# Splitting the modulated tokens where they are produced, and loading them in ten split slots

## The chip, the core and the metric

The kernel runs on one NeuronCore of a Trainium2 chip. The metric is the time of one execution in microseconds on the device. A core has five engines that run their own instruction lists in order and wait for each other by semaphores: TensorE (PE, matrix products), VectorE (DVE), ScalarE (ACT), GpSimd (POOL) and SyncE (SP). In this kernel SP issues every DMA, and it too works through one list in order: an issue that waits holds back all issues behind it.

## The reference

Two layers over 2048 latent tokens and 256 context tokens of 1024 features, in float32:

```python
for i in range(DEPTH):
    ml = layer_norm(xl) * (1.0 + sc_l) + sh_l          # the same for the context tokens
    parts = split(ml @ w_in[i])                        # one wide projection
    oa = gdn_branch(...)   # gated DeltaNet: short convolution, gates, chunked scan in both directions
    ob = na_branch(...)    # neighbourhood attention on a 64 wide grid
    oc = gla_branch(...)   # gated linear attention in both directions
    y = concat(norm(oa) * silu(z_a), ob * silu(z_b), norm(oc) * silu(z_c)) @ w_out[i]
    xl = layer_norm(alpha * xl + gate * y) * ln_g[i] + ln_b[i]
```

## The kernel before

The 2304 tokens (context first) are 18 tiles of 128 tokens, or 6 blocks of 384 (BLK). M, the normalised and modulated tokens, transposed to features by tokens, is the input of the projection. It lies in DRAM, one tensor M0 to M5 for each block, float32, 128 partitions by 8 feature slices (KD) by 384 tokens. `modulate` makes a tile of it: PE transposes the normalised tile (L165), ACT scales and shifts it into `m` (L168), and a DMA stores `m` (L170). In layer 0 that is a stage of its own ahead of the projection (`stage_p1`); for layer 1 the output stage of layer 0 (`Out.run`) calls it after each of its tiles.

The projection needs more precision than one pass of TensorE in float32r gives, so each operand is split in a leading part with float32r's significand and the rest, and three products are summed (`dense_mm`, L202). The class `Dense` streams M five times for each layer: pass 1 with the columns of GLA (while GLA's blocks run), pass 2 with those of the neighbourhood attention, passes 3 and 4 with keys, queries and values of two heads of DeltaNet each (the conv passes: a convolution of five taps on DVE, L654, then SiLU and layouts), pass 5 with DeltaNet's z columns (while the scan is being set up). In each pass `Dense.block` loads a block in four raw tiles of two feature slices and splits each of them: ACT makes the leading part `mh` (L191), POOL or DVE in turn the rest `ml` (L194). There are two slots for raw tiles and four for each of the parts, so that one block fills all of the split slots:

```python
raw = pool.tile([128, 2, BLK], F32, tag="mraw", name="mraw")        # two slots
nc.sync.dma_start(raw, self.M[b][:, 2 * h:2 * h + 2])
for lst, tag in ((mh, "mh"), (ml, "ml")):
    lst.append(pool.tile([128, 2, BLK], F32R, tag=tag, name=tag, bufs=4))
split_(e, mh[h], ml[h], raw, nc.scalar, nc.vector if h % 2 else nc.gpsimd)
```

The order of the instructions of every engine is set when the kernel is built, by a scheduler that works with estimated times and priorities; the splits have a high priority. Memory is handed out by pools; a pool that is opened where another one lay waits for that one's last work. The weights' raw tiles (`raw`, L229) are split likewise (`wh`, `wl`).

## Time and profile before

| what | value |
|---|---|
| median of 3 runs | 4035.41 us |
| the 3 runs | 4031.47, 4035.41, 4062.93 us |
| span of the profiled execution | 4030.6 us |
| busy: PE, PEld, DVE, ACT, POOL | 90%, 78%, 69%, 46%, 28% of the span |
| mean granted TensorE clock | 0.905 of full speed |
| DMA moved | 674.38 MB, 167 GB/s on average |
| layer 0: pass 1, pass 2 | 73 to 326 us, 326 to 668 us |
| layer 0: conv passes | 668 to 903 us, 903 to 1122 us |
| layer 0: pass 5, scan and attention, output stage | 1122 to 1290, 1290 to 1810, 1810 to 2140 us |
| layer 1: pass 1, pass 2 | 2140 to 2342 us, 2342 to 2681 us |
| layer 1: conv passes, pass 5 | 2681 to 2906, 2906 to 3088, 3088 to 3250 us |

The profiled execution's span, first to last instruction, is 4030.6 us; the time of an execution has a little more around it: the fastest of the three runs is 0.9 us longer than this span, and the median 4.8 us longer. The stages are cut where the loads of a pass's blocks begin; stages overlap at the cuts. Busy shares are means over stages with different limits, so what counts is which wait ends last within a stage.

### The profile page before, as it was taken

What the parts mean: (1) busy time and instruction counts of PE and PEld (TensorE: products, weight loads), DVE (VectorE), ACT (ScalarE), POOL (GpSimd) and SP (SyncE); (2) the same over time, 40 slices, a digit from 0 to 9 for tenths busy, and PEclk for the clock granted to TensorE, in tenths of its full rate; (3) what the DMA queues carried; (4) which work ended last, traced back from release to release, by engine and by line L of the source; (5) the groups of instructions that cost most, each with busy time, mean ns of one, the idle gap of its engine ahead of it and who ended that gap; (6) DMA issues with size and microseconds to landing.
All of it is one profiled execution on the core that took longest, in us unless ns stands there. A gap on an engine that the chain in (4) does not pass through costs nothing.

```text
span 4030.6 us, 77205 instructions
## 1 busy us (share of the span) xinstructions
PE 3609.5 (90%) x27270; PEld 3133.3 (78%) x27270; DVE 2765.4 (69%) x7584; ACT 1847.2 (46%) x4628; POOL 1142.5 (28%) x1334
## 2 busy tenths in 40 slices
PE   5999999888998999997898989998899989889788
PEld 2777778877887888996676768887898778879676
DVE  7455653899987667447776466438999865754587
ACT  6534322456543544546555342324565434445442
POOL 2121212554223322321332121125324231232133
PEclk6979879899999978998899887999999987989899
DMA  8523226654566868666545232266554776785743
GB/s 285 163 75 118 82 70 186 171 170 145 167 202 193 243 193 224 213 188 210 176 140 167 88 98 70 91 194 170 161 159 146 247 218 178 212 229 164 230 146 110
DMA packets 646265, 674.38 MB, mean 167 GB/s; under 512 B 184830, under 2 KB 524662, under 8 KB 645878
## 3 DMA queue, kind: packets, MB, share of 16 engines
q1 hardware_dynamic: 645878, 669.44, 55.2%
q8 instruction: 216, 3.54, 0.4%
q14 instruction: 171, 1.40, 0.1%
HBM read 472.98 MB, written 196.28 MB: 166 GB/s over the span
## 4 chain that ended last, share of the span: by engine, by line
PE 42%; DVE 26%; DMA 16%; ACT 6%; issue 5%; POOL 2%; SPq 2%; DVEq 0%; ACTq 0%; POOLq 0%
PE p L202 18%; DVE acc L654 5%; PE p L1250 3%; DMA gb<-GR 2%; PE py L202 2%; DMA raw<-in_w_in 2%; DMA mraw<-M 2%; PE pv L1015 1%; PE pd L1022 1%; PE po L1035 1%; DVE mix L1356 1%; DMA OA<-o 1%; PE pk L1004 1%; PE pA L491 1%; DVE gb L858 1%
## 5 line engine op out<-in xcount | busy, mean ns | idle before, releaser
L202 PE MATMUL p<-ml,wh 128*128 128x384 f32 (+1 forms) x1824 | 648.9, 356 | 49.7 <-POOL ml L194 35.2
L202 PE MATMUL p<-mh,wh 128*128 128x384 f32 (+1 forms) x1824 | 644.3, 357 | 33.6 <-ACT mh L191 9.9
L202 PE MATMUL p<-mh,wl 128*128 128x384 f32 (+1 forms) x1824 | 639.9, 351 | 0.6 <-DVE wl L194 0.6
L194 POOL TENSOR_TENSOR ml<-mraw,mh 128x768 fp32r<-128x768 f32 x120 | 248.7, 2072 | 632.6 <-ACT mh L191 602.1
L202 PEld LDWEIGHTS p<-ml,wh 128*128 128x128 f32 (+1 forms) x1824 | 354.8, 195 | 80.5 <-POOL ml L194 45.4
L654 DVE SCALAR_TENSOR_TENSOR acc<-pre,cw,acc 128x384 f32<-128x384 f32 (+1 forms) x576 | 400.4, 712 | 15.1 <-ACT acc L652 12.2
L202 PEld LDWEIGHTS p<-mh,wh 128*128 128x128 f32 (+1 forms) x1824 | 353.4, 195 | 64.1 <-ACT mh L191 15.8
L202 PEld LDWEIGHTS p<-mh,wl 128*128 128x128 f32 (+1 forms) x1824 | 354.9, 195 | 12.3 <-issue 1.6
L202 PE MATMUL p<-wh,mh 128*128 128x512 f32 (+1 forms) x848 | 343.9, 406 | 14.2 <-DVE zt L1266 9.3
L202 PE MATMUL p<-wl,mh 128*128 128x512 f32 (+1 forms) x848 | 340.0, 401 | 5.5 <-DVE wl L194 5.5
L202 PE MATMUL p<-wh,ml 128*128 128x512 f32 (+1 forms) x848 | 341.8, 405 | 1.8 <-POOL ml L194 1.6
L191 ACT CAST mh<-mraw 128x768 fp32r<-128x768 f32 x240 | 197.9, 833 | 140.0 <-DMA mraw<-M 109.1
L202 PE MATMUL py<-wh,mh 128*128 128x512 f32 x544 | 222.4, 410 | 17.6 <-ACT mh L1365 14.4
L202 PE MATMUL py<-wl,mh 128*128 128x512 f32 x544 | 218.3, 402 | 0.3 <-DVE wl L1303 0.3
L202 PE MATMUL py<-wh,ml 128*128 128x512 f32 x544 | 213.4, 404 | 4.3 <-DVE ml L1366 4.3
L997 POOL TENSOR_TENSOR kd<-kk,eD 128x256 f32<-128x256 f32 x144 | 90.1, 627 | 437.0 <-DMA kk<-KK 147.3
L202 PEld LDWEIGHTS p<-wh,mh 128*128 128x128 f32 x848 | 164.9, 195 | 53.0 <-DVE zt L1266 12.1
L202 PEld LDWEIGHTS p<-wh,ml 128*128 128x128 f32 x848 | 165.0, 195 | 40.0 <-POOL ml L194 3.1
L202 PEld LDWEIGHTS p<-wl,mh 128*128 128x128 f32 x848 | 165.5, 195 | 38.8 <-DVE wl L194 6.0
L1388 POOL TENSOR_TENSOR y<-y,g 128x1024 f32<-128x1024 f32 x32 | 77.0, 2408 | 412.5 <-ACT y L1387 412.5
L194 DVE TENSOR_TENSOR ml<-mraw,mh 128x768 fp32r<-128x768 f32 x120 | 134.8, 1123 | 71.8 <-ACT mh L191 71.7
L1229 ACT ACTIVATE w<-w,mn 128x696 f32<-128x696 f32 (+2 forms) x136 | 112.9, 831 | 135.6 <-DVE mn L1226 135.0
(323 smaller groups left out, 8947.5 us busy)
## 6 DMA issues: line engine op xcount, KB each, us to landing
mraw<-M SPq DMA_DIRECT2D x240, 384.0 KB
kk<-KK SPq DMA_DIRECT2D x144, 512.0 KB
raw<-in_w_in SPq DMA_DIRECT2D x104, 256.0 KB
w<-in_w_mod SPq DMA_DIRECT2D x96, 256.0 KB
M<-m SPq DMA_DIRECT2D x36, 512.0 KB
KK<-kq SPq DMA_DIRECT2D x96, 192.0 KB
KK<-kvt SPq DMA_DIRECT2D x48, 384.0 KB
kq<-KK SPq DMA_DIRECT2D x72, 256.0 KB
```

The source lines that it names most:

```text
L191: eng_hi.copy(hi, src)
L194: eng_lo.tensor_tensor(lo, src, hi.bitcast(F32), op=ALU.subtract)
L202: e.nc.tensor.matmul(p, x(k), y(k), start=n == 0, stop=n == 3 * KD - 1)
L491: nc.tensor.matmul(pA[jb * s:jb * s + s, i, ib * s:ib * s + s], KQ[s][hs, 0, t0 + jb * s:t0 + jb * s + s], KQ[s][hs, 1, t0 + ib * s:t0 + i ...
L654: nc.vector.scalar_tensor_tensor(acc[:, :n], pre[:, k:k + n], w(kind, k), acc[:, :n], op0=ALU.mult, op1=ALU.add)
L858: nc.vector.scalar_tensor_tensor(E[:, d, h], gb[:, d, h], self.G[:, d, c, h0 + h:h0 + h + 1], e.mats[:, 1 + d], op0=ALU.subtract, op1=ALU.min)
L997: nc.gpsimd.tensor_tensor(kd, kv[:, :, 0], self.eD[:, d, c, h0:h0 + 2].unsqueeze(2).to_broadcast([128, 2, 128]), op=ALU.mult)
L1004: nc.tensor.matmul(pk[:, h], kq[:, h, 0], S[:, h], start=True, stop=True)
L1015: nc.tensor.matmul(pv[:, h], X[:, h], R[:, h], start=True, stop=True)
L1229: nc.scalar.activation(w[:, a, 0:256 + nk], w[:, a, 0:256 + nk], AF.Exp, bias=m[:, a:a + 1], scale=-1.0, accum_out=sm[:, a:a + 1])
L1250: nc.tensor.matmul(p[:, a], l, r, start=j == 0, stop=j == len(parts) - 1)
L1388: eng.tensor_tensor(y[:, s], y[:, s], self.g[:, 0, s], op=ALU.mult)
```

## The change

`modulate` now splits its tile: ACT copies each half of `m` to a float32r tile `mhi`, POOL subtracts that from `m` in place, and two DMAs store the two parts. M has a second axis for the parts. `Dense.block` loads the finished parts slice by slice, both parts of a feature slice in one load, into ten slots; nothing is split in the passes. The other lines of the diff only drop comments.

```diff
@@ modulate
-    nc.sync.dma_start(M[b][:, :, o:o + 128], m)
+    h = P.tile([128, KD, 128], F32R, tag="mhi", name="mhi")
+    l = m.bitcast(F32R)
+    for q in range(2):
+        s = slice(4 * q, 4 * q + 4)
+        nc.scalar.copy(h[:, s], m[:, s])
+        nc.gpsimd.tensor_tensor(l[:, s], m[:, s], h[:, s].bitcast(F32), op=ALU.subtract)
+    nc.sync.dma_start(M[b][:, 0, :, o:o + 128], h.bitcast(F32))
+    nc.sync.dma_start(M[b][:, 1, :, o:o + 128], m)
@@ Dense.block
-        mh, ml = [], []
-        for h in range(4):
-            raw = pool.tile([128, 2, BLK], F32, tag="mraw", name="mraw")
-            nc.sync.dma_start(raw, self.M[b][:, 2 * h:2 * h + 2])
-            for lst, tag in ((mh, "mh"), (ml, "ml")):
-                lst.append(pool.tile([128, 2, BLK], F32R, tag=tag, name=tag, bufs=4))
-            with e.tc.high_priority(PRI):
-                split_(e, mh[h], ml[h], raw, nc.scalar, nc.vector if h % 2 else nc.gpsimd)
-        return mh, ml
+        m = []
+        for k in range(KD):
+            m.append(self.mp.tile([128, 2, BLK], F32R, tag="mm", name="mm", bufs=MBUF))
+            self.e.nc.sync.dma_start(m[k].bitcast(F32), self.M[b][:, :, k])
+        return m
@@ Dense.run
-                dense_mm(e, p, lambda k: wh[:, k], lambda k: wl[:, k], lambda k: mh[k // 2][:, k % 2], lambda k: ml[k // 2][:, k % 2])
+                dense_mm(e, p, lambda k: wh[:, k], lambda k: wl[:, k], lambda k: m[k][:, 0], lambda k: m[k][:, 1])
@@ Layer.__init__
-        self.M = [d.tile([128, KD, BLK], F32, name=f"M{b}") for b in range(NB)]
+        self.M = [d.tile([128, 2, KD, BLK], F32, name=f"M{b}") for b in range(NB)]
```

The slots take as much memory as before (two raw and eight split tiles of 3 KB for each partition, now ten of 3 KB); the pools of `stage_p1` and of the output stage grow by the two buffers of `mhi`, 8 KB for each partition. The scheduler makes a new order of the whole program from this. Three places of it follow.

First place: SP's list at the start of layer 0, after the first stores of M. M_70 to M_75 are the six blocks of M; `raw` are raw weights; x is the input. Before:

```order
L170 DMA M_70<-m 1024x1x128
L179 DMA x<-in_x 128x1024
L229 DMA raw<-in_w_in 128x4x128 x2
L170 DMA M_71<-m 1024x1x128
L229 DMA raw<-in_w_in 128x4x128
L240 DMA mraw<-M_70 128x768 x2
L229 DMA raw<-in_w_in 128x4x128
L170 DMA M_71<-m 1024x1x128
```

SP's list of the changed kernel, where these weights (128x4x128: columns of k and q; 128x256: of v and z) now stand:

```order
L176 DMA M_75<-mhi 128x8x128
L177 DMA M_75<-m 128x8x128
L393 DMA b2c<-in_gla_b 128x2x1
L391 DMA w2p<-in_gla_w 16x128 x2
L237 DMA raw<-in_w_in 128x4x128 x4
L406 DMA rp<-in_rope 128x768
L410 DMA rc<-RC 32x384
L237 DMA raw<-in_w_in 128x256 x16
```

The loads of the weights of k, q, v and z have moved from between the first tiles' stores to behind the stores of the last tile of the last block.

Second place: PE's list at the start of layer 0. L165 are the transposes of `stage_p1`, eight for each tile; 48x384 is the first column group of pass 1, 128x384 those of k and q. Before:

```order
L165 MATMUL p<-ident,xn 128x128 x56
L202 MATMUL p<-mh,wh 48x384
L202 MATMUL p<-mh,wh 128x384
L202 MATMUL p<-ml,wh 48x384
L202 MATMUL p<-mh,wl 48x384
L202 MATMUL p<-mh,wh 48x384
```

PE's list of the changed kernel, from the end of the first column group of block 0 (the first group stands behind 44 transposes and between 12 more):

```order
L209 MATMUL p<-mm,wh 48x384 x2
L209 MATMUL p<-mm,wl 48x384
L372 MATMUL pt<-ident,r_1336 128x48 x3
L165 MATMUL p<-ident,xn 128x128 x88
L209 MATMUL p<-mm,wh 128x384 x2
L209 MATMUL p<-mm,wl 128x384
```

Before, products of k stood behind the transposes of seven tiles, and those of the other eleven tiles among the products; now all 144 transposes stand ahead of the first product of k.

Third place: DVE's list in the second conv pass of layer 0 (acc: convolution taps; ml: the split; X, A, xd: set-up of the scan). Before:

```order
L879 STREAM_TRANSPOSE xd<-X 32x192 x4
L654 SCALAR_TENSOR_TENSOR acc<-pre,cw,acc 128x384
L659 SCALAR_TENSOR_TENSOR vb<-th,acc 128x2
L659 SCALAR_TENSOR_TENSOR vb<-th,acc 128x382
L682 COPY kvt<-p 128x3x128
L654 SCALAR_TENSOR_TENSOR acc<-pre,cw,acc 128x384 x3
L659 SCALAR_TENSOR_TENSOR kq<-th,acc 128x2
L659 SCALAR_TENSOR_TENSOR kq<-th,acc 128x382
L687 TENSOR_SCALAR nv<-ss 128x6
L654 SCALAR_TENSOR_TENSOR acc<-pre,cw,acc 128x384
L194 TENSOR_TENSOR ml<-mraw,mh 128x768
```

DVE's list of the changed kernel in the same pass:

```order
L883 STREAM_TRANSPOSE xd<-X 32x192 x4
L867 SCALAR_TENSOR_TENSOR X<-pk,nW,gb 128x128
L658 SCALAR_TENSOR_TENSOR acc<-pre,cw,acc 128x384
L867 SCALAR_TENSOR_TENSOR X<-pk,nW,gb 128x128
L658 SCALAR_TENSOR_TENSOR acc<-pre,cw,acc 128x384
L869 TENSOR_TENSOR A<-pk,gb 128x256
L867 SCALAR_TENSOR_TENSOR X<-pk,nW,gb 128x128 x2
L663 SCALAR_TENSOR_TENSOR vb<-th,acc 128x2
L663 SCALAR_TENSOR_TENSOR vb<-th,acc 128x382
L658 SCALAR_TENSOR_TENSOR acc<-pre,cw,acc 128x384
```

The split is gone from between the taps. On SP's list the loads of a block in the passes now stand as two slices early and six in a row, each of which waits for PE to have read its slot for the last time.

## Rows read from the trace of the kernel before

**Rows 1.** Windows by stage: engines' busy us (instructions), granted clock, DMA share, GB/s.

```profile
668.00:903.00 235.00, 206.06 (x1056) 185.13 (x1055) 193.78 (x376) 110.68 (x256) 108.44 (x112) 0.92 0.65 179
903.00:1122.00 219.00, 195.67 (x1082) 177.73 (x1082) 203.85 (x530) 123.99 (x304) 79.10 (x83) 0.97 0.51 152
1810.00:2140.00 330.00, 275.48 (x1302) 225.14 (x1300) 251.92 (x785) 186.85 (x593) 85.21 (x36) 0.92 0.55 177
2681.00:2906.00 225.00, 199.00 (x1046) 181.13 (x1046) 182.38 (x368) 103.72 (x244) 94.93 (x101) 0.95 0.60 168
2906.00:3088.00 182.00, 175.10 (x1014) 168.48 (x1013) 174.99 (x517) 109.50 (x269) 54.89 (x58) 0.99 0.49 144
```

**Rows 2.** Chain of waits by line, conv passes: 668:903, 903:1122, 2681:2906, 2906:3088.

```profile
by line: DVE acc L654 26.8%; DMA raw<-in_w_in 11.7%; issue 8.1%; PE p L202 7.9%; DVE kq L659 5.5%; DVE nry L60 4.0%; DVE wl L194 3.6%; ACT acc L652 2.7%; DVE vb L659 2.6%; ACT wh L191 2.1%; DVE ml L194 2.1%; DVE nk L689 1.8%; DVE nra L58 1.
by line: DVE acc L654 21.6%; PE p L202 14.1%; issue 11.0%; DMA gb<-GR 5.7%; DVE ml L194 3.8%; DVE nry L60 3.7%; DVE vb L659 3.4%; POOL ml L194 2.9%; DVE nra L59 2.5%; ACT jk L685 2.5%; DVE kq L659 2.4%; DVE wl L194 2.2%; ACT kvt L697 2.1%; 
by line: PE p L202 23.4%; DVE acc L654 18.5%; issue 8.0%; DMA raw<-in_w_in 6.7%; DVE kq L659 4.6%; DMA tr<-RZ 3.7%; DVE wl L194 2.9%; DVE ml L194 2.4%; SPq L1123 2.3%; DVE vb L659 2.2%; POOL tb L1126 1.9%; ACT acc L652 1.8%; DMA w<-in_w_mod
by line: DVE acc L654 26.1%; issue 12.4%; PE p L202 12.3%; DMA mraw<-M 3.9%; DVE kq L659 3.8%; DVE ml L194 3.0%; DVE X L863 2.7%; DVE M L919 2.5%; DVE vb L659 2.4%; DVE gb L858 2.2%; DVE nry L60 1.9%; DMA gb<-GR 1.8%; ACT jk L685 1.8%; DVE 
```

**Rows 3.** Chain of waits by line: 73:326, 326:668, 1122:1290, 2140:2342, 2342:2681.

```profile
by line: PE p L202 52.1%; PE pA L491 4.7%; DMA mraw<-M 4.5%; PE p L165 2.6%; POOL ml L194 2.6%; PE pO L525 2.5%; POOL qkp L469 2.3%; ACT m L168 2.3%; DMA M<-m 2.2%; DVE a L446 2.1%; issue 2.0%; PE pD L473 1.8%; PE pB L498 1.8%; DVE a L441 1
by line: PE p L202 37.8%; issue 4.9%; PE pD L473 3.7%; PE pA L491 3.6%; PE pO L525 3.1%; DVE a L446 3.1%; POOL qkp L469 2.8%; DMA mraw<-M 2.8%; POOL ml L194 2.5%; DVE a L442 2.2%; PE pO L523 2.0%; PE pB L498 1.9%; DVE a L441 1.6%; DMA OC<-o
by line: PE p L202 45.0%; DMA gb<-GR 7.7%; DMA mraw<-M 7.4%; issue 3.8%; DVE gb L858 3.6%; DVE X L863 3.1%; DVE acc L654 2.7%; DVE xd L879 2.3%; PE pz L935 2.3%; DVE A L865 2.0%; PE px L941 1.5%; DVE tmp L918 1.4%; PE pq L675 1.4%; DVE M L9
by line: PE p L202 37.5%; DMA mraw<-M 5.3%; POOL ml L194 4.7%; issue 4.4%; PE pA L491 2.7%; ACT mh L191 2.6%; DVE a L446 2.6%; DMA raw<-in_w_in 2.4%; PE pD L473 2.3%; DVE a L441 2.3%; DVE A L511 2.2%; POOL qkp L469 2.1%; PE pO L525 1.7%; DV
by line: PE p L202 35.1%; DMA o<-OC 4.2%; PE pD L473 3.9%; DMA OC<-o 3.9%; DMA mraw<-M 3.6%; issue 3.6%; PE pA L491 3.5%; PE pO L525 2.9%; DVE a L446 2.7%; DVE G L508 2.5%; DVE A L511 2.5%; DVE a L442 2.0%; DVE a L441 1.8%; DVE a L443 1.7%;
```

**Rows 4.** Tile mraw: the splits, ns min/median/max, first and last start us.

```profile
L191 ACT CAST mh<-mraw x240: 814/834/879, 79.9 to 3236.8; 128x768 fp32r<-128x768 f32 x120
L194 POOL TENSOR_TENSOR ml<-mraw,mh x120: 1799/1846/6107, 80.9 to 3235.2; 128x768 fp32r<-128x768 f32 x120
L194 DVE TENSOR_TENSOR ml<-mraw,mh x120: 935/948/2595, 81.6 to 3238.5; 128x768 fp32r<-128x768 f32 x120
```

**Rows 5.** Timeline of POOL, then DVE, in layer 1's second conv pass: start us, us.

```profile
2933.34 2.30 POOL L194 TENSOR_TENSOR ml<-mraw,mh 128x768 fp32r<-128x768 f32 x1 [1.40 <-ACT mh L191]
...
2933.86 2.19 DVE L654 SCALAR_TENSOR_TENSOR acc<-pre,cw,acc 128x386 f32<-128x386 f32 x1
...
2936.59 0.61 DVE L654 SCALAR_TENSOR_TENSOR acc<-pre,cw,acc 128x386 f32<-128x386 f32 x1
```

**Rows 6.** Chain of waits in order of time, 0 to 135 us: start us, us.

```profile
58.03 4.56 DMA M<-m
...
70.94 5.64 DMA M<-m
...
76.69 2.90 ACT m L168 x8
...
83.33 5.16 PE p L202 x21
...
126.87 3.19 DMA mraw<-M
```

**Rows 7.** Groups kept apart by shape: count, busy us, mean ns.

```profile
L194 POOL TENSOR_TENSOR wml<-w,wmh 128x512 fp32r<-128x512 f32 x80 | 120.7, 1511 | 61.5 <-ACT wmh L191 41.4 <-ACT pre L645 11.0 <-ACT mh L191 3.2
L191 ACT CAST wmh<-w 128x512 fp32r<-128x512 f32 x96 | 59.0, 616 | 28.8 <-DMA w<-in_w_mod 11.1 <-POOL wml L194 8.8 <-DVE wml L194 5.4
```

**Rows 8.** DMA: GB/s in 40 slices of the span; an issue's size.

```profile
GB/s 285 163 75 118 82 70 186 171 170 145 167 202 193 243 193 224 213 188 210 176 140 167 88 98 70 91 194 170 161 159 146 247 218 178 212 229 164 230 146 110
...
M<-m SPq DMA_DIRECT2D x36, 512.0 KB
```

**Rows 9.** Longest pieces of the chain, whole span: a run of dense products.

```profile
3033.64 12.41 PE p L202 x70
```

More of the change, by code (lines that the diff above doesn't have):

```diff
@@ L206 @@
 PRI = 100000
+MBUF = 10
 class Dense:
@@ L235, in block @@
     def block(self, b):
-        e, nc, pool = self.e, self.e.nc, self.mp
-        mh, ml = [], []
-        for h in range(4):
-            raw = pool.tile([128, 2, BLK], F32, tag="mraw", name="mraw")
-            nc.sync.dma_start(raw, self.M[b][:, 2 * h:2 * h + 2])
-            for lst, tag in ((mh, "mh"), (ml, "ml")):
-                lst.append(pool.tile([128, 2, BLK], F32R, tag=tag, name=tag, bufs=4))
-            with e.tc.high_priority(PRI):
-                split_(e, mh[h], ml[h], raw, nc.scalar, nc.vector if h % 2 else nc.gpsimd)
-        return mh, ml
+        m = []
[3 more added lines that the diff above has]
+        return m
     def run(self, wp, chan, tok, bufs=1, after=None, width=None, raws=4, tw=None, w0=None):
@@ L262, in run @@
         for b in range(NB):
-            mh, ml = nxt if b == 0 else self.block(b)
+            m = nxt if b == 0 else self.block(b)
             for (wh, wl, wd), cb in cw:
                 p = ps.tile([wd, BLK], F32, tag="dn", name="p")
-                dense_mm(e, p, lambda k: wh[:, k], lambda k: wl[:, k], lambda k: mh[k // 2][:, k % 2], lambda k: ml[k // 2][:, k % 2])
+                dense_mm(e, p, lambda k: wh[:, k], lambda k: wl[:, k], lambda k: m[k][:, 0], lambda k: m[k][:, 1])
                 with e.tc.high_priority(PRI):
@@ L274, in run @@
                     s = slice(t * 128, (t + 1) * 128)
-                    dense_mm(e, p, lambda k: mh[k // 2][:, k % 2, s], lambda k: ml[k // 2][:, k % 2, s], lambda k: wh[:, k, :wd], lambda k: wl[:, k, :wd])
+                    dense_mm(e, p, lambda k: m[k][:, 0, s], lambda k: m[k][:, 1, s], lambda k: wh[:, k, :wd], lambda k: wl[:, k, :wd])
                     with e.tc.high_priority(PRI):
```

## Prediction

> **What bounds the kernel now.** I read the windows by stage first, to see in each which engine is full; then the chain of waits for the same windows, to see which waits end last; then the rows of the splits themselves and what they disturb; and last the start, in order of time. The windows show the conv passes to be DVE's: it is busy for 194 of 235, 204 of 219, 182 of 225 and 175 of 182 us [rows 1], and the convolution's taps alone hold 27, 22, 19 and 26% of their chains [rows 2]. Passes 1, 2 and 5 are PE's: dense products hold 35 to 52% of the chain [rows 3]. The splits stand on these chains, but in small pieces, and the start of layer 0, where M is made, is on PE's way as a whole: the first run of dense products begins at 83.3 us, behind the first stores of M [rows 6].
>
> **The change part by part.**
>
> *A. The splits in the passes go.* 240 casts, 120 POOL and 120 DVE subtractions leave [rows 4]. What counts is their share of the chain. Conv passes: DVE's ml has 2.1% of 235, 3.8% of 219, 2.4% of 225 and 3.0% of 182 us, that is 4.9 + 8.3 + 5.4 + 5.5 = 24.1 us, and POOL's ml 2.9% of 219 = 6.4 us [rows 2]; together 30.5 us. Passes 1 and 2: POOL's ml has 2.6% of 253, 2.5% of 342 and 4.7% of 202 us, 6.6 + 8.6 + 9.5 = 24.7 us, and ACT's mh 2.6% of 202 = 5.3 us [rows 3]; together 30.0 us. Names below the cut of these rows are not counted. In sum 60.5 us. In the conv passes PE is next: 36 groups of 24 products are 864, at 12.41 us for 70 [rows 9] 153 us, against windows of 182 to 235 us, so each pass could give 29 us or more before PE binds.
>
> *B. POOL no longer holds DVE up.* A POOL split ran from 2933.34 for 2.30 us; the tap that began at 2933.86 took 2.19 us where the one at 2936.59 took 0.61 [rows 5]. It lost 1.58 us. The four conv passes have 48 such POOL splits, so DVE may get back anything from 0 to 48 x 1.58 = 76 us. Of DVE's 755 us there [rows 1] the named DVE pieces of the chain hold 46.4% of 235, 39.6% of 219, 30.6% of 225 and 44.6% of 182 us, 346 us [rows 2], or 46%. I take that share, 35 us; it is nearer to the row than either end.
>
> The rule behind this is in the Trainium skill, page "SBUF — State Buffer", section "Who interferes with whom": a VectorE instruction with two SBUF inputs and a GpSimd instruction that reads SBUF exclude each other, and the later one waits for the whole of the other. This trace agrees: POOL's split ended at 2935.64 and the tap at 2936.05 [rows 5]. The rule speaks against the change too, since the new subtractions run on POOL; that is a rival below.
>
> *C. The loads double.* 240 loads of 384 KB become 480. No load has a split behind it, but two slices of a block are loaded ahead and six wait for PE to have read their slots; before, two raw tiles, half a block, were ahead. SP waits with them, and the stores of keys and values, the raw weights and the scan's rows queue behind. Loads have 4.5% of 253, 2.8% of 342, 7.4% of 168, 5.3% of 202, 3.6% of 339 and 3.9% of 182 us of the chain, 11.4 + 9.6 + 12.4 + 10.7 + 12.2 + 7.1 = 63.4 us [rows 2, 3]. Between the last read of a slot and the first use of its new content stand some 30 products on PE's list, 5.3 us at the rate above [rows 9], and a load took 3.19 us when it was alone [rows 6]. So most are covered. From below, the 63 us could vanish; from above, double. I take no change: the cover is longer than the load, but six in a row share the queues.
>
> *D. The output stage of layer 0.* Each of 18 tiles gets two casts of 0.62 us and two POOL subtractions of 1.51 us [rows 7], and a second store of 512 KB [rows 8]. ACT is busy for 187 of 330 us there, DVE for 252 [rows 1]. Casts cost between 0 and 18 x 1.23 = 22 us; the subtractions, by holding DVE, between 0 and 36 x 1.51 = 54 us. ACT idles for 43% of the time and POOL's ends are off the way, so I take 15 us, near the lower end.
>
> *E. The start of layer 0.* This is where order counts. Before, the weights of k, q, v and z were loaded between the first tiles' stores, and PE took up dense products after seven tiles. Now SP issues these weights behind the store of the last tile, and PE's list has all 144 transposes ahead of k's first product. The cover that is lost: eleven tiles of `stage_p1` ran beside dense products. The first store was issued at 58.03 us [rows 6]; the first low part now comes a cast pair and a subtraction later, at 58.0 + 1.2 + 1.5 = 60.8 us. A tile's pace: `m` has two buffers, each held for 2.90 us of writing, 1.23 of casts, 1.51 of subtraction and a store of 4.56 to 5.64 us [rows 6, 7], 10.2 to 11.3 us, so a tile every 5.1 to 5.6 us. By bytes it is the same: an input and two stores of 512 KB are 1.57 MB, 5.5 us at the 285 GB/s of the first slice, the most that the trace shows [rows 8]. Seventeen more tiles end at 148 to 157 us; a weight's load of 3.2 us and its split of about 1.2 us later k can begin, at 152 to 161 us against 83.3 us. That is 69 to 78 us late. What comes back: in pass 1, ACT's m, the stores of M and the transposes hold 2.3 + 2.2 + 2.6% of 253 us, 18 us of the chain [rows 3], which then lie in the wait. E costs 51 to 60 us, taken as 55.
>
> Sum: - 60.5 - 35 + 0 + 15 + 55 = - 25.5 us, 4005 us of span. The profiled span, 4030.6 us, is 4.8 us below the median of the runs, 4035.4 us, and I lay the sum on the median: 4010 us. At this kernel 1%, 40 us, is about what a measurement can tell from no change.
>
> **The rivals.**
>
> *The gain without the loss.* If PE's late start is mostly made up, because pass 1 then runs with ACT, DVE and the queues to itself, E falls to about 20 us, and if DVE's relief comes whole (76 us, B's upper end), the sum is - 60.5 - 76 + 15 + 20 = - 101 us: 3934 us. For it speaks that DVE is at 93 and 96% in two conv passes [rows 1] and that a waiting DVE also delays what frees buffers; against it that pass 1 is PE's own [rows 3] and what PE has not done by 155 us it must do later. Half of this, about 3970 us, still counts as faster. Chance 0.33.
>
> *Slower: the loads become the block's edge.* Six slices wait on PE, 2.36 MB. If at each of the 50 edges within passes the first group of columns stands for one bare load of 3.19 us [rows 6], that is 160 us in place of the 63 that the chain has now, 97 us more than C: 4107 us. It decides when six loads need longer than PE's cover of some 5.3 us for a slot; the conv passes already move 144 to 179 GB/s [rows 1] of the 285 seen [rows 8]. Against it: SP issues slices as slots come free one by one, not all at the end. Chance 0.15.
>
> *The new subtractions hold DVE in the output stage.* As a mechanism of this kernel: 36 POOL subtractions of 1.51 us [rows 7] fall in a stage where DVE is busy for 76% of the time [rows 1]; if each stops one two-input instruction as the tap was stopped [rows 5], D is 54 + 11 = 65 us in place of 15, and the time 4060 us. Against it: the subtraction comes at the end of a tile's work, and the scheduler runs tiles beside each other. Chance 0.10. This is what the rule of the Trainium skill named above would make of D.
>
> **How the numbers follow.** The forecast, 4010 us, has 0.42 with its own range of 3985 to 4040 us, which also holds the neighbourhood of no change. The range for 8 in 10 reaches from 3950 us, inside the first rival, to 4075 us, short of the second's price, and takes in the bounds of C and of E. Faster by over 1% (below 3995 us): the first rival and the lower part of the forecast's own spread, 0.36. Slower by over 1% (above 4076 us): the second rival and a little of the third, 0.16. Within 1%: 0.48.
>
> **What would show it.** In the new trace the first run of dense products of k should begin at 150 to 160 us, with PE nearly idle from 80 us on, and pass 2 of layer 0 should begin some 55 us later than at 326 us. The conv passes should each be 10 to 25 us shorter, with taps near 0.61 us and no split on DVE or POOL. Loads of `mm` should hold about 60 us of the chain. The output stage of layer 0 should be 0 to 30 us longer. The prediction is wrong if the start costs less than 40 us, if the loads hold over 120 us of the chain, or if the conv passes keep their length although DVE has less to do.

## The result and the profile after

The changed kernel takes 4143.2 us (median of 4126.1 to 4159.6), the kernel before, run beside it, 4033.4 us: a ratio of 1.028, 95% interval 1.023 to 1.033. By the ratio it is 113 us slower, where 25 us less was forecast, and it lies above the range. The profiled execution has a span of 4157.8 us.

I read the windows first, by the stages of [rows 1]: the start (80:160, 160:404), the four conv passes, and the output stage of layer 0 (1914:2238).

```profile
80.00:160.00 80.00, 33.57 (x126) 21.65 (x124) 31.36 (x70) 50.97 (x131) 34.51 (x27) 0.54 0.87 263
160.00:404.00 244.00, 225.75 (x2299) 182.23 (x2300) 127.12 (x329) 75.58 (x138) 33.72 (x26) 0.87 0.44 135
731.00:958.00 227.00, 204.14 (x1038) 183.21 (x1037) 155.59 (x340) 83.36 (x214) 80.06 (x96) 0.91 0.70 203
958.00:1160.00 202.00, 192.10 (x1088) 180.29 (x1087) 171.21 (x485) 104.91 (x275) 52.37 (x72) 0.97 0.68 214
2775.00:2988.00 213.00, 190.70 (x1010) 173.11 (x1009) 156.72 (x343) 85.35 (x214) 71.58 (x88) 0.95 0.77 225
2988.00:3164.00 176.00, 174.33 (x1043) 171.64 (x1042) 163.11 (x550) 97.51 (x263) 24.00 (x49) 1.00 0.67 210
1914.00:2238.00 324.00, 263.27 (x1215) 214.33 (x1215) 253.15 (x748) 186.38 (x585) 120.85 (x63) 0.91 0.61 191
```

The conv passes did become shorter: 235, 219, 225 and 182 us before, now 227, 202, 213 and 176. DVE's busy time in them fell from 755 to 647 us, and PE, busy for 90, 95, 90 and 99% of them, is now the fuller engine. In the start PE is busy for 34 of 80 us while the queues move 263 GB/s. The tile view of M and PE's timeline, both of layer 0's start, show why (stores with ns min/median/max, first and last start; then start us, us):

```profile
L176 SPq DMA_DIRECT2D M<-mhi x18: 359/360/2820, 56.4 to 160.3; - x18
```

```profile
155.48 1.11 PE L165 MATMUL p<-ident,xn 128*128 128x128 f32 x4 [0.28 <-ACT m L168]
168.92 1.01 PE L209 MATMUL p<-mm,wh 128*128 128x384 f32 x2 [12.33 <-ACT wh L198]
```

A tile of M takes (160.3 - 56.4) / 17 = 6.1 us, and k's first product comes at 168.9 us, behind its weight's split. Before, it came at 81 us, the second of the two products with which PE's timeline begins at 80.88 us; the 83.3 us of [rows 6] are where the chain's first run of products begins. Next come, of the page, the taps' group and the products of the weights' leading part with both parts of M; then, of the view of the tile `mm`, the idle time until a slice landed (us, times). That view adds up PE and its weight loads, PEld, which stand still side by side; PE alone stood still for 43.6 us, 46 times:

```profile
L658 DVE SCALAR_TENSOR_TENSOR acc<-pre,cw,acc 128x384 f32<-128x384 f32 (+1 forms) x576 | 382.1, 683 | 30.1 <-ACT acc L656 24.1
L209 PE MATMUL p<-mm,wh 128*128 128x384 f32 (+1 forms) x3648 | 1002.3, 355 | 69.3 <-DMA mm<-M 36.6
```

```profile
  DMA mm<-M: 112.9, 121
```

And the mean granted clock is 0.884, before 0.905. It has two levels, 1.2 and 2.4 GHz; an estimate from the means is that 23.2% of 4158 us, 965 us, ran at the lower one, before 19.0% of 4031, 766 us.

Where the time goes shows when the same instructions are matched in both traces (the k-th transpose, gate, tap or output product of one with the k-th of the other). This table gives how much later they start than in the kernel before, in us, as the median of those within 12 us of a place (us in the trace before); the kernels below "after" are the experiments of the next section.

| kernel | 320 pass 2 | 740 conv | 1110 conv ends | 1400 scan | 1660 scan | 1710 scan | 1850 output | 2110 layer 1 | 2760 conv | 3080 conv ends | 3250 scan | 4010 end |
|---|---|---|---|---|---|---|---|---|---|---|---|---|
| after | +64 | +67 | +50 | +67 | +64 | +98 | +99 | +107 | +94 | +73 | +93 | +127 |
| e1 weights early | -38 | +17 | +3 | +31 | +16 | +37 | +32 | +53 | +45 | +30 | +52 | +42 |
| e2 memory alone | +60 | +39 | +40 | +57 | +42 | +67 | +68 | +80 | +83 | +84 | +91 | +87 |
| e4 early, half loads | -29 | +14 | -8 | -8 | -37 | -10 | -14 | 0 | -19 | -49 | -48 | -42 |
| e7 early, 8 slots | -37 | +22 | +23 | +34 | +20 | +38 | +36 | +51 | +62 | +63 | +86 | +85 |
| e8 three parts stored | -41 | +89 | +73 | +88 | +82 | +119 | +117 | +181 | +188 | +173 | +172 | +174 |
| e9 pass 2 stores | -1 | +24 | +1 | +14 | -5 | +32 | +29 | +31 | +44 | +30 | +35 | +39 |
| e12 reordered | +10 | +16 | +20 | +18 | -2 | +34 | +31 | +36 | +38 | +38 | +33 | +46 |
| e13 before again | -4 | 0 | +2 | +4 | +9 | +9 | +12 | +15 | +13 | +14 | +15 | -4 |
| e14 rest not awaited | -35 | -3 | -29 | -37 | -55 | -26 | -31 | -17 | -30 | -58 | -54 | -68 |
| e19 parts apart | -27 | +25 | +13 | +16 | +7 | +30 | +25 | +44 | +51 | +39 | +48 | +36 |

After: 67 us late when the conv passes begin, 17 us back in them, then 49 lost in pass 5 and the scan of layer 0 and 8 in its output stage, 13 back in passes 1 and 2 of layer 1 and 21 in its conv passes, and 54 lost in its pass 5, scan and output stage. In both scans and the output stage of layer 1 the change has edited nothing. Two cautions: e13 is a second execution of the kernel before, and it too strays by up to 15 us; and where two chains run beside each other, a place follows one of them. At 320 us GLA's products are 48 us late in e1 and 133 us late in e8, though the gates are early; from 1400 to 1710 us the table follows the scan's state products, not attention's. So there were three questions: what holds the start, what the loads cost, and why untouched stages lose.

### The profile page after: what moved, and what is told of

It is laid out like the page before. It is cut to its first block, busy times and chain, and to the rows that moved or that the text cites. A ratio compares the mean times of both kernels' runs of the same rounds, so it can differ in the third digit from the quotient of the medians.

```text
span 4157.8 us, 77171 instructions
## 1 busy us (share of the span) xinstructions
PE 3678.0 (88%) x27270; PEld 3193.6 (77%) x27270; DVE 2610.7 (63%) x7464; ACT 1705.8 (41%) x4458; POOL 971.8 (23%) x1286
## 5 line engine op out<-in xcount | busy, mean ns | idle before, releaser
L209 PE MATMUL p<-mm,wh 128*128 128x384 f32 (+1 forms) x3648 | 1002.3, 355 | 69.3 <-DMA mm<-M 36.6
L209 PEld LDWEIGHTS p<-mm,wh 128*128 128x128 f32 (+1 forms) x3648 | 674.3, 194 | 126.2 <-DMA mm<-M 57.5
L209 PE MATMUL p<-mm,wl 128*128 128x384 f32 (+1 forms) x1824 | 635.2, 350 | 3.3 <-DVE wl L201 3.3
L209 PE MATMUL p<-wh,mm 128*128 128x512 f32 (+1 forms) x1696 | 566.4, 407 | 21.3 <-DVE zt L1270 9.1
L209 PEld LDWEIGHTS p<-wh,mm 128*128 128x128 f32 x1696 | 329.0, 196 | 102.3 <-DVE zt L1270 12.6
L658 DVE SCALAR_TENSOR_TENSOR acc<-pre,cw,acc 128x384 f32<-128x384 f32 (+1 forms) x576 | 382.1, 683 | 30.1 <-ACT acc L656 24.1
L209 PEld LDWEIGHTS p<-mm,wl 128*128 128x128 f32 (+1 forms) x1824 | 353.3, 194 | 17.2 <-DVE wl L201 4.5
L209 PE MATMUL p<-wl,mm 128*128 128x512 f32 (+1 forms) x848 | 342.2, 404 | 8.1 <-DVE wl L201 8.1
L209 PEld LDWEIGHTS p<-wl,mm 128*128 128x128 f32 x848 | 166.4, 196 | 41.9 <-DVE wl L201 9.3
L1254 PE MATMUL p<-v,wl 120*128 120x64 f32 (+1 forms) x960 | 148.6, 295 | 0.0
L922 DVE TENSOR_TENSOR tmp<-M 96x30 f32<-96x30 f32 (+4 forms) x360 | 127.8, 355 | 27.0 <-issue 20.7
```

Source lines behind the costliest of these rows:

```text
L209: e.nc.tensor.matmul(p, x(k), y(k), start=n == 0, stop=n == 3 * KD - 1)
L658: nc.vector.scalar_tensor_tensor(acc[:, :n], pre[:, k:k + n], w(kind, k), acc[:, :n], op0=ALU.mult, op1=ALU.add)
L922: nc.vector.tensor_tensor(tv, col, row, op=ALU.mult)
L1254: nc.tensor.matmul(p[:, a], l, r, start=j == 0, stop=j == len(parts) - 1)
```

## The experiments

Ratios are to the kernel before, run beside each; 1% is 40 us.

**e1, e2: the start.** `stage_p1`'s pool grows by `mhi`, 8 KB per partition. e1 gives `mhi` there the buffers of the normalised tokens; e2 gives the kernel before the memory alone.

```diff
e1 (after)   -    h = P.tile([128, KD, 128], F32R, tag="mhi", name="mhi")
             +    h = P.tile([128, KD, 128], F32R, tag="mhi" if act else "xn", name="mhi")
e2 (before)  +    h = P.tile([128, KD, 128], F32, tag="mhi", name="mhi")
             +    nc.gpsimd.memset(h[:, 0, 0:1], 0.0)
```

> The changed kernel, but in the input stage of layer 0 the new leading part of M takes the buffers that the normalised tokens already have there, so the stage's memory does not grow and no longer lies over the weights' buffers; everything else is as in the changed kernel. Theory 1 (the main loss is that the weights of k, q, v and z wait for the memory of the whole input stage): k's first products come at 85 to 95 us instead of about 170, and the time is 60 to 95 us below the changed kernel's, 4050 to 4083 us; the doubled loads and the scan keep what is left of the loss. Rival (the doubled loads of M are the main loss, and the start is only made up for later or replaced by another wait): k's products come early as well, but the time is within 25 us of the changed kernel's, 4120 us or more.

> The kernel before, with one thing added: a tile of 4 KB per partition, two buffers, in the stages that make M, which nothing uses but a store of one element. So the memory of the input stage grows as in the change, and no split moves. Theory 1: the weights wait for the end of the input stage here too, k's products come at 140 us or later, and the time is 45 to 95 us above the kernel before, 4080 to 4130 us. Rival (the late start costs nothing by itself, since pass 1 runs faster behind it): 4025 to 4050 us.

e1: 4082 us, 1.0106 (1.0052 to 1.0160); e2: 4109 us, 1.0175 (1.0126 to 1.0224). In e1's timeline k's products begin with the first group's:

```profile
91.63 0.99 PE L209 MATMUL p<-mm,wh 128*48 128x384 f32 x2
...
92.73 0.84 PE L209 MATMUL p<-mm,wh 128*128 128x384 f32 x2
```

In e2's timeline they come at 132 us, somewhat earlier than the 140 us expected:

```profile
132.09 0.69 PE L204 MATMUL p<-mh,wh 128*128 128x384 f32 x1 [9.32 <-ACT wh L193]
```

Both times of execution fit theory 1: it is the memory, not the split, that puts the weights behind the whole input stage. The pool that grew lies over the weights' buffers, and what lies there must be read before a weight can land. It is worth 1.0280 - 1.0106 = 1.7%, 70 us, and still e1 is slower than before. By the table, 50 of the 70 us stand where the conv passes begin (+67 against +17). The rest comes behind 3250 us, where the two kernels differ only in their order, so it need not be the memory's.

**e3, e4: half loads.** A pass loads only the leading part and uses it for the rest; e4 has e1's line too.

```diff
-            m.append(self.mp.tile([128, 2, BLK], F32R, tag="mm", name="mm", bufs=MBUF))
-            self.e.nc.sync.dma_start(m[k].bitcast(F32), self.M[b][:, :, k])
+            m.append(self.mp.tile([128, 2, BLK], F32R, tag="mm", name="mm", bufs=MBUF)[:, 0:1].to_broadcast([128, 2, BLK]))
+            self.e.nc.sync.dma_start(m[k][:, 0].bitcast(F32), self.M[b][:, 0, k])
```

> The changed kernel, but a pass loads only the leading part of each slice and uses it in place of the rest too, so that the bytes loaded are those of the kernel before; the rest of M is left out of the products. All else stays, the late start too. Theory 2 (the doubled bytes cost 20 to 60 us: at the block's edges, and by delaying the scan's set-up in pass 5, where the changed kernel moves 284 GB/s): the time is 20 to 60 us below the changed kernel's, 4083 to 4123 us, and pass 5 of layer 0 loses nothing more against the kernel before. Rival (the loads are covered, and what is lost in pass 5 and in the scan comes from the order of the instructions and from TensorE's clock): within 12 us of the changed kernel, 4131 to 4155 us.

> The two edits together: the input stage's memory does not grow, and a pass loads only the leading part of each slice (the rest of M is left out of the products). Against the kernel before this leaves the splits out of the passes at no cost in bytes loaded. If theories 1 and 2 hold and add, the time is the changed kernel's less both, 3950 to 4020 us, below the kernel before, which would be the gain of the splits alone that the prediction had put at 60 to 95 us, less the output stage's 15. Rival (the scan and the output stages lose some 30 to 50 us by themselves in the changed order): 4030 us or more.

e3: 4015 us, 0.9956 (0.9929 to 0.9984); e4: 3983 us, 0.9871 (0.9821 to 0.9920). The second half of the loads costs 3.2% (131 us) with the weights late and 2.35% (95 us) with them early, where theory 2 had allowed 60 us at most. In e4's view of `mm`, the idle time of PE and PEld until a slice landed, then in e1's (PE alone: 27.7 and 45.2 us):

```profile
  DMA mm<-M: 65.8, 56
```

```profile
  DMA mm<-M: 112.7, 111
```

**e5, e6: pieces, and pass 5.** e5 is e1 with M as `[128, KD, 2, BLK]`, so that a load takes 3 KB in one piece from a partition; e6 is e1 with half loads in pass 5 alone.

> The kernel with the weights early (4082 us), and M laid out so that the two parts of a slice stand side by side: a load takes 3 KB in one piece from each partition instead of two pieces of 1.5 KB; the stores keep their pieces of 512 bytes. Bytes are the same, the loads' pieces are half as many. Theory 2a (the number of pieces makes the doubled loads dear): it gets back a good part of the 99 us that lie between full and half loads, 30 to 80 us, 4000 to 4050 us, and a load's issue on SP falls from 0.56 us to below 0.45 us. Theory 2b (bytes, that is the queues' throughput and the slots, make them dear): within 15 us of 4082 us.

> The kernel with the weights early, and only pass 5 of each layer (the gate columns z, beside the set-up of the scan) loads the leading part alone and uses it for the rest too; the rest of M is left out of the products of that pass. It saves 37.7 of 377 MB of loads, a fifth of what half loads in all passes save. Theory 2c (the doubled loads are dear where they meet the scan's set-up): 35 us or more of the 99 come back, 4047 us or less. Theory 2d (they cost about the same in every pass): a fifth, 20 us, 4055 to 4070 us. Rival (pass 5's loads are covered): within 10 us of 4082 us.

e5: 1.0087 (1.0061 to 1.0114), 8 us off e1 and inside its interval, although a load's issue fell from 0.56 to 0.38 us. So it is not the pieces, nor SP's time. e6: 1.0107 (1.0061 to 1.0154), no gain: theory 2c fell. (The expectation misstates the bytes: it saves 18.9 of 189 MB of loads, by the counts of the DMA lines; the fifth is right.) I had read pass 5's 284 GB/s in the changed kernel (1160 to 1320 us) as the place of the loss.

**e7, e11: slots.** `MBUF = 8` in place of 10, in e1 and in e4.

> The kernel with the weights early, with eight slots for slices in place of ten: exactly one block, and a slice of the next block can be loaded only when PE has read the one in its place. Theory 2e (what the loads cost is the wait for slots at the edge between blocks): the wait grows by two slices at each of 50 edges, 1 to 2 us each, 50 to 100 us more than with ten slots, 4130 to 4180 us. Rival (throughput binds, not slots): at most 20 us more, below 4105 us.

> The kernel with the weights early and half loads (the rest of M is left out of the products), with eight slots in place of ten. With full loads two slots less cost 1.5%, 60 us. Theory 2f (what a load costs at a block's edge is its time on the queues, 384 KB or 192 KB, behind the slot's release): two slots less cost half as much or less here, 0 to 30 us, a ratio of 0.987 to 0.995 to the kernel before. Rival 2g (it is a fixed time of each load, whatever its bytes): 45 to 75 us again, a ratio of 0.998 to 1.006.

e7: 4123 us, 1.0255 (1.0204 to 1.0305), 60 us more than e1, as theory 2e had it. e11: 3985 us, 0.9864 (0.9817 to 0.9911), no more than e4. The idle time of PE and PEld for slices, e7's and e11's (PE alone: 82.4 and 47.2 us):

```profile
  DMA mm<-M: 185.7, 188
```

```profile
  DMA mm<-M: 105.0, 99
```

Slots matter with whole slices only. But the idle time itself is not the price: PE alone has 20 us more of it in e11 than in e4 and nothing is lost, and 37 us more in e7 than in e1 and 60 are lost.

**e8, e9: other places for the split.** In e8 the producer stores M raw and in both parts, and only the conv passes load finished parts; in e9 the producer is left alone and pass 2 stores the parts that it splits.

```diff
e9 +            if store:
   +                nc.sync.dma_start(self.S[b][:, 0, 2 * h:2 * h + 2], mh[h].bitcast(F32))
   +                nc.sync.dma_start(self.S[b][:, 1, 2 * h:2 * h + 2], ml[h].bitcast(F32))
```

> The kernel before, with M stored in three parts, raw, leading and rest. Passes 1, 2 and 5 load raw slices and split them as before; only the four conv passes load finished parts, into the same ten slots in turn. The input stage's memory does not grow. If the gain lies in the conv passes, where DVE binds (40 to 60 us by the runs so far), and the cost of the loads in the other passes, above all in pass 5, it is below both kernels: the conv passes give 45 us back, their doubled loads take about 25, the output stage of layer 0 takes 15 to 20 with its third store, 4005 to 4030 us. Rival (the doubled loads cost as much in the conv passes as the splits did): 4035 us or more.

> The kernel before, in which the producer is left alone: M is stored raw, passes 1, 2 and 5 load it raw and split it, and pass 2 also stores its two parts, which the four conv passes then load as finished parts into the same ten slots in turn. In the run that stored three parts at the producer the conv passes gave 30 + 16 us and all that was lost lay where M is made (+75 and +80 us). Theory: with the producer left alone the conv passes give 35 to 45 us and the 48 stores of pass 2 in each layer cost 0 to 15 us, so 3990 to 4015 us, 0.992 of the kernel before. Rival (the stores hold the slots and SP's queue in pass 2 as long as the conv passes give back): 4030 us or more.

e8: 4198 us, 1.0416 (1.0379 to 1.0453); e9: 4077 us, 1.0115 (1.0062 to 1.0168). Both theories missed and the times are the rivals', though not because of the conv passes, which give 16 + 15 us in e8 and 23 + 14 in e9 between the table's places. e8 pays where M is made: its last store of M in layer 0 goes at 272.9 us, before at 152.9, it is 89 us late by the conv passes, and loses 64 us in layer 0's output stage. e9 pays 25 us in pass 2 and 28 us from the end of the conv passes to 1850, in pass 5 and the scan, which it does not touch.

**e12, e13: the order.** e12 is the kernel before with one line in `modulate`, which leaves the mathematics and the passes as they are; e13 is the kernel before, for a second trace.

```diff
+    if not act:
+        nc.gpsimd.memset(m.rearrange("p k t -> p (k t)"), 0.0)
```

> The kernel before, and in the input stage of layer 0 POOL fills each tile m once before ACT writes it: 18 stores of about 1 us by an engine that waits there anyway, and nothing of the change. The weights stay early. But it moves the list by which the instructions of the scan and of the output stages are put in order: about as many of them stand elsewhere as in the kernel with the memory alone. Theory 3 (a part of the loss, some 30 to 40 us in the scan and the output stages, comes from another order there, and the order of the kernel before is a good one): 20 to 45 us above the kernel before, a ratio of 1.005 to 1.011, with the loss behind 1300 us. Rival (another order costs nothing on the whole, and those losses are chance or follow from the loads): within 10 us of the kernel before.

> The kernel before, unchanged, for a second trace of it. Theory 3 expects the stretch of the scan between 1660 and 1720 us, which ran at full clock in the first trace and in which nearly all other kernels lose 15 to 37 us, to be the same again, within 10 us. Rival (it was a lucky draw of TensorE's clock in that one execution): the stretch is 15 us or more longer.

e12: 4080 us, 1.0090 (1.0056 to 1.0124), 36 us; e13: the stretch from 1660 to 1710 is the same again (+9 at both ends), so the first trace was no lucky execution there. The order did change: of the 4628 products that PE runs between 1290 and 1815 us, compared by the names of their tiles, e13 has every one at its old place in PE's list, e12 460. The 18 fills take 17 us of POOL, and e12's last store of M goes at 154.9 us, 2 us later than before, so they are hardly the price. A new order alone, then, cost this kernel some 36 us. The expectation had put them behind 1300 us, into the scan and the output stages, and the table does not bear that out. e12 is 20 us late when the conv passes end and loses 11 more up to 1850, where e13 loses 10. The step from -2 to +34 between 1660 and 1710 is that of the state products alone; attention's products beside them go from +17 to +25. The windows of the kernel before, then of e12, over the whole scan and over that stretch:

```profile
1290.00:1815.00 525.00, 489.69 (x4630) 454.56 (x4628) 309.81 (x997) 257.98 (x707) 150.11 (x315) 0.90 0.73 212
1576.00:1660.00 84.00, 79.09 (x788) 72.27 (x788) 46.79 (x145) 40.49 (x119) 28.36 (x65) 0.81 0.82 225
1620.00:1660.00 40.00, 38.06 (x359) 35.33 (x359) 18.09 (x57) 18.59 (x55) 17.93 (x42) 0.87 0.70 203
1660.00:1690.00 30.00, 30.00 (x375) 27.57 (x374) 9.86 (x33) 17.13 (x48) 8.34 (x16) 1.00 0.79 259
1690.00:1720.00 30.00, 30.00 (x262) 29.36 (x262) 13.52 (x42) 18.94 (x52) 8.06 (x14) 1.00 0.50 151
```

```profile
1310.00:1847.00 537.00, 488.35 (x4710) 454.24 (x4708) 307.43 (x992) 261.08 (x715) 150.85 (x315) 0.91 0.74 207
1600.00:1660.00 60.00, 52.33 (x500) 47.68 (x500) 36.12 (x119) 27.41 (x79) 12.46 (x25) 0.91 0.86 223
1660.00:1684.00 24.00, 20.81 (x238) 19.68 (x238) 8.18 (x24) 11.08 (x32) 13.34 (x32) 0.79 0.83 248
1684.00:1720.00 36.00, 36.00 (x296) 33.28 (x295) 5.57 (x16) 15.12 (x41) 3.20 (x9) 0.57 0.30 96
```

Before, PE stands still for 4.9 of 84 us and then runs at 1.00; in e12 it stands still for 7.7 of 60 and 3.2 of 24 us and then runs at 0.57 while full. The changed kernel has a like stretch: 57 us at 0.61 from 1723. But the kernel before has its slow stretch just ahead, 0.81, and over the whole scan the clock is 0.90 before and 0.91 in e12: in these two the low clock falls elsewhere, there is not more of it.

**e15, e16, e14, e17: bytes or order.** e15 and e16 are e1 and e4 with e12's line. e14 is e4, and the rest is loaded too, into tiles that nothing reads. e17 is the kernel before with a copy of 384 KB within DRAM behind each load.

```diff
e14 +            u = self.mp.tile([128, 1, BLK], F32, tag="mu", name="mu", bufs=MBUF)
    +            self.e.nc.sync.dma_start(u[:, 0], self.M[b][:, 1, k])
e17 +            nc.sync.dma_start(self.U[self.n % 8], self.M[b][:, 2 * h:2 * h + 2])
```

> The kernel with the weights early and full loads (1.0106 of the kernel before), with POOL filling each tile m once in the input stage, which moves the order of the scan. If the order is a lottery in which this kernel had an average draw, it stays within 20 us, a ratio of 1.006 to 1.016; if the order was its main loss, the ratio falls below 1.002.

> The kernel with the weights early and half loads (0.987 of the kernel before; the rest of M is left out of the products), with the same filling of m and so another order of the scan. If the bytes make the difference between full and half loads, it stays near 0.987, at most 0.995; if that kernel only had a lucky order, as the kernel before has, it rises by 30 us or more, to 0.996 or above, and the price of the bytes shrinks as much.

> The kernel with the weights early and half loads (3983 us, 0.987 of the kernel before), and each rest is loaded too, into a tile of its own that no product reads, so all the bytes of the change are moved, in twice as many loads, but PE waits for the leading parts alone (the rest of M is left out of the products). Theory 2h (it is the bytes on the queues, which delay everything that is loaded or stored beside them): 50 to 100 us more than with half loads, a ratio of 1.000 to 1.012. Theory 2f (it is the turnaround of a slot, release, load of 384 KB and PE's wait): at most 25 us more, a ratio of 0.987 to 0.993.

> The kernel before, and behind each of its 240 loads of a raw pair of slices the same 384 KB are copied within DRAM to a place that nothing reads: as many bytes on the queues as the change adds to the loads, and nothing waits for them. Theory 2h (bytes on the queues): 50 to 110 us more than the kernel before, a ratio of 1.012 to 1.027, of which some 36 us may be the order. Theory 2f (the slots' turnaround): what another order costs, 0 to 40 us, a ratio of 1.000 to 1.010.

e15: 1.0157 (1.0109 to 1.0206); e16: 0.9768 (0.9733 to 0.9802), even better than e4. So the half loads' gain was no lucky order; another order moves these kernels by +20 and -41 us, and the gap between full and half is 157 us here. e14: 3965 us, 0.9810 (0.9776 to 0.9844): nothing more than with half loads, as theory 2f had it. But it does not decide against theory 2h, for the scheduler put the loads that nothing reads elsewhere: all 240 of layer 0 stand ahead of 400 us, where e14's own loads of the leading part go on to 1226 us, and those of layer 1 ahead of 2334 us. The view of `mu` in e14, up to 1500 us and behind it:

```profile
L250 SPq DMA_DIRECT2D mu<-M x240: 319/428/1839, 87.5 to 381.4; - x120
...
L250 SPq DMA_DIRECT2D mu<-M x240: 319/430/1598, 1911.4 to 2333.8; - x120
```

So e14 shows that the bytes cost nothing in pass 1, though its queues moved 320 GB/s from 80 to 400 us and e4's 169. In the passes behind that its queues have no more to do than e4's: in layer 0's second conv pass 172 GB/s (905 to 1090 us), e4's 171, e1's 213. e17: 1.0147 (1.0110 to 1.0185), 59 us, of which a new order may be 36; its copies too stand in those early stretches, 74 to 316 and 1982 to 2347 us, and it does not decide.

**e18, e19: what is awaited.** e18 loads and awaits whole slices and lets PE read the leading part twice; e19 is e14 with the rest read as it should be, so it computes everything.

```diff
e18 +            u = self.mp.tile([128, 2, BLK], F32R, tag="mm", name="mm", bufs=MBUF)
    +            m.append(u[:, 0:1].to_broadcast([128, 2, BLK]))
    +            self.e.nc.sync.dma_start(u.bitcast(F32), self.M[b][:, :, k])
e19 +            m.append([self.mp.tile([128, BLK], F32R, tag=t, name=t, bufs=MBUF) for t in ("mm", "mu")])
    +            for x in range(2):
    +                self.e.nc.sync.dma_start(m[k][x].bitcast(F32), self.M[b][:, x, k])
```

> The kernel with the weights early, with whole slices loaded and awaited in whole slots, but the products read the leading part for the rest too (the rest of M is left out of the products). Theory 2f (the wait for whole slices and the turnaround of whole slots is what costs): as with full loads, a ratio of 1.004 to 1.016 to the kernel before. Theory 2i (what costs is that PE reads a second operand, and the half-load kernels were fast because it read one twice): 0.975 to 0.992.

> The kernel with the weights early, but the two parts of a slice are loaded by two transfers into tiles of their own, ten slots of half the size for each, and both are read as they should be: nothing is left out. Theory 2f: PE can begin with the leading part, a slot comes free for half a slice, and most of the 95 us come back, a ratio of 0.980 to 0.998, below both kernels. Theory 2i: as with full loads in whole slots, 1.004 to 1.016.

e18: 1.0123 (1.0089 to 1.0157): theory 2i fell, the operand is not what costs. PE reads the same operands in e14, and the two differ by 126 us. e19: 4058 us, 1.0072 (1.0044 to 1.0099): finer slots give back little, 14 us against e1, so theory 2f's hope for them was wrong. e14 and e19 move the same bytes in as many loads, but e19 loads the rest with the leading part, in every pass. Of e14: PE's busy time and the DMA line of its page, PE's own waits for slices (us, times, longest), and the window of layer 0's second conv pass; then the same of e19, with the waits for `mu`, the rest's tiles:

```profile
PE 3563.2 (90%) x27270; PEld 3113.0 (79%) x27270; DVE 2602.1 (66%) x7464; ACT 1700.0 (43%) x4458; POOL 959.4 (24%) x1286
...
DMA packets 787388, 787.70 MB, mean 199 GB/s; under 512 B 196926, under 2 KB 696502, under 8 KB 786998
...
PE p L209 <- DMA mm<-M: 28.3, 25, 3.6
...
905.00:1090.00 185.00, 178.82 (x1042) 168.12 (x1042) 167.39 (x505) 98.79 (x262) 40.04 (x65) 1.00 0.56 172
```

```profile
PE 3616.3 (89%) x27270; PEld 3140.9 (77%) x27270; DVE 2589.2 (64%) x7464; ACT 1704.5 (42%) x4458; POOL 964.2 (24%) x1286
...
DMA packets 787390, 787.72 MB, mean 194 GB/s; under 512 B 196926, under 2 KB 696502, under 8 KB 786998
...
PE p L209 <- DMA mm<-M: 37.8, 30, 7.4
...
PE p L209 <- DMA mu<-M: 22.0, 27, 4.1
...
935.00:1125.00 190.00, 184.05 (x1049) 171.62 (x1048) 169.92 (x510) 98.80 (x260) 47.54 (x64) 0.98 0.67 213
```

That the rest is loaded and awaited in every pass costs 2.6%, 106 us. Of the 103 us between the two spans, 53 are the same 27270 products taking longer (3616.3 against 3563.2 us), where two executions of the kernel before differ by 18 us in PE's busy time. The other 50 are pauses of PE, of which 31.5 are waits for a slice (59.8 against 28.3 us). The other four pairs, after and e3, e1 and e4, e15 and e16, e18 and e4, give the same picture: products that take 40 to 90 us longer, 43 to 81 us more of pauses, and only 17 to 20 us of them waits for a slice.

The mean granted clocks go with it: 0.909, 0.909, 0.903 and 0.903 in e14, e16, e4 and e11, and 0.898, 0.894, 0.885, 0.896 and 0.897 in e19, e18, e15, e1 and e7. Between e14 and e19 that is an estimated 721 against 829 us at the lower level; half of the difference, 54 us, is near the 53 us by which the products became longer. So about half of the price comes as products at the lower clock. That the pauses lower the clock is a reading and not shown: no run changes one without the other.

Nor does any pair of runs part the wait from the bytes that the queues move in the same passes. Two runs speak for the wait: e7 moves e1's bytes and waits longer for slots, at 60 us, and e6 takes bytes from pass 5 and gains nothing. That whole slices hold SP longer is not what costs: its loads of `mm` wait for PE for 180 us in e1 and 195 in e4.

No version that computes all products beats the kernel before; e19 is the nearest.

## Why the prediction was wrong, point by point

**The step that failed is C**, "I take no change: the cover is longer than the load". Five pairs give the price of the awaited second half: after and e3, 131 us; e1 and e4, 95; e15 and e16, 157; e18 and e4, 102; e19 and e14, 106. The bounds, -63 to +63 us, were also too narrow. The cover of 5.3 us and the load of 3.19 us [rows 6, 9] came from one load that was alone; the forecast had the right objection, six loads in a row share the queues, and gave it no price. The second rival had it at 97 us more, 4107 us, and 0.15; by e7 and e11 its mechanism, the slot's turnaround, is part of it. But both looked for the price in PE's waits for slices, and these grow by only 17 to 32 us; what was missing is that the same products take 40 to 90 us longer at a lower mean clock. What joins the two, whether bytes beside the waits have a part, and why e11's extra waits cost nothing, stays open. The sign that was named for C, the loads' share of the chain, cannot be read: the chain that the trace after gives begins at 4120 us.

**A, B and D** were right as a sum, though each of the kernels that show it has an order of its own. The kernels that do all of the change but await half the bytes, with the weights early, are at 0.987, 0.981 and 0.977: -52, -77 and -94 us; the forecast for these parts was -80.5. In the conv passes e4 and e14 gain 52 and 54 us (table, 740 to 1110 and 2760 to 3080) where A and B had 65.5; the changed kernel keeps 38. The cap that A named, PE, was misjudged: 153 us of dense products for a pass left out PE's other work, and the rows had PE at 175 of 182 us [rows 1]. B, as DVE's time, was more than 35 us: in the windows of the conv passes DVE is busy for 108 us less, of which its own 48 splits are 48 us, so some 60 us came back to its other work. The taps have a part of it, 400.4 us before and 382.1 after in all passes. That the passes gained less than DVE did fits with PE being the fuller engine now. The page before has:

```profile
L654 DVE SCALAR_TENSOR_TENSOR acc<-pre,cw,acc 128x384 f32<-128x384 f32 (+1 forms) x576 | 400.4, 712 | 15.1 <-ACT acc L652 12.2 <-issue 0.7
```

D, 15 us, was near: between 1850 and 2110 the changed kernel loses 8 us, e4 and e14 14, e19 19 and e1 21, of which the reordered e12, which adds nothing there, has 5. The third rival, 65 us, falls with it: the new subtractions run there, and DVE is busy for 253 us in that stage where it was for 252. It is what the Trainium skill's rule on shared access (page "SBUF — State Buffer", section "Who interferes with whom") would have made of D.

**E** was right in kind, and 55 us lies in what was measured: 70 us by after and e1, 34 by e3 and e4, 71 less a part for the order by e2. Its parts were off: a tile takes 6.1 us, not 5.1 to 5.6, and k starts at 168.9, not 152 to 161 us, so that it is 88 us late and not 69 to 78. And its cause was not named: the pool's 8 KB, which one tag avoids.

**Not in the forecast at all** is the price of a new order. An edit makes the scheduler order the untouched stages anew, and e12 lost 36 us so. From the end of the conv passes to 1850, mostly the scan, the changed kernel loses 49 us, e1 29, e2 28, e12 11, and e13, the same kernel again, 10, while e4 and e14 lose nothing; behind the conv passes of layer 1 the changed kernel loses 54 us and e1, with the same loads, 12. So orders and waits both have a part in the changed kernel's loss there, and the runs do not say how much. A price of that size, set beside the other bounds, would have widened the forecast's range.

In two smaller places the working slips: half of the first rival's gain of 101 us gives 3985 us, not 3970, and the 3.2 us for a weight's load in E are the row of a raw tile of M.

In sum: about -77 for the splits with D (e14), +106 for the awaited rest (e19 less e14), +70 for the start: +99 us, against 113 measured. That it comes so near is partly the choice of pairs; the others would give anything from +35 to +175 us.

## What to carry to other kernels

Before trading recomputation for loads, price the loads in the stages where the consumer awaits them: six loads in a row were 95 to 157 us here, where one load alone had looked covered. An experiment that leaves out the wait may move the load too, since a scheduler is free to put it elsewhere; look in the trace when it was issued before you read the result. A tile added to a pool can move the loads of whatever the pool lies over; look at the order of the loads first, and lend it a tag that is free. And where a scheduler makes the order, reorder the old kernel once without a change, to know what a new order alone costs.

## What the runs showed of the hardware

The same products take longer in kernels whose PE waits for more: 3616.3 us in e19 against 3563.2 in e14, at a mean granted clock of 0.898 against 0.909. The order moves the slow stretches: in the scan of e12, after PE had stood still for 10.9 of 84 us, the clock was 0.57 for 36 us though PE was full; in the kernel before, after 4.9 of 84 us at 0.81, it was 1.00, as in its second trace; over the whole scan it was 0.91 in e12 and 0.90 before. Halving the number of pieces of a load cut its issue on SP from 0.56 to 0.38 us and moved the time by no more than its uncertainty (e5). And 94 MB more, 788 in place of 693, loaded early in each layer, cost nothing measurable (0.981 in e14 against 0.987 and 0.977 without them), though the queues moved 320 GB/s from 80 to 400 us where they moved 169 without them.
